# Experts' loop of a DeepNorm encoder layer: every engine held to program order, with splits, sums and weights laid out in a software pipeline

## The chip, the cores and the metric

One core of a Trainium2 chip runs the whole kernel. The metric is the time of one execution on the device in microseconds (us), lower is better. PE (TensorE) multiplies, DVE (VectorE) and ACT (ScalarE) work on tiles, POOL (GpSimd) issues DMAs and small copies, SP (SyncE) issues DMAs.

## What is computed

One encoder layer over 512 positions of 2048 features: adaptive modulation, two kinds of attention, and a retrieval of experts (PEER). The change touches the last part alone:

```python
def peer(h, wq, keys, u_tab, v_tab):            # tables: 16384 experts x 2048
    ...                                          # 8 heads choose 16 experts each: et, gt
    a = jnp.einsum('td,thkd->thk', xt, u_tab[et])
    w = gt * jax.nn.gelu(a, approximate=False)
    return jnp.einsum('thk,thkd->td', w, v_tab[et])
...
x = layer_norm(DN_ALPHA * x + g2 * p, ln2_g[l], ln2_b[l])
```

## The kernel before

Each of the 512 positions takes 128 of the 16384 experts, and the kernel computes this in two ways side by side. For 352 positions (TD, the matmul's columns) it goes densely through all experts: **u product** of a block of 128 experts (16 row blocks of the table, 3 matmuls each since every operand is split into a high and a low half of reduced precision: 48 matmuls), Gelu, times the dense weights, then **v product** into 16 sums of 128 x 352 (accT in SBUF). For the other 160 positions it gathers rows: one indirect DMA brings 128 rows of 2048 values (1 MB, a *row* tile), DVE multiplies and sums it (L1058 for u, L1064 for v).

Experts come in 32 groups of 4 blocks (GE = 4). The u products of 56 blocks are made in the stages before; their Gelu values lie in DRAM (ga_d). The experts' loop then runs over n = 0 to 18: for group gorder[n] (14 to 31) it makes the 4 u products, and between them the 4 v products (j = 0 to 3, 512 output features each) of the group before it: "u, v, u, v, ...". This is the **u/v part**. After it the v products of groups 0 to 13 remain (the **v-only part**, code under the pool "fin"); the last, 13, has another shape and flows into the final normalization. Between the two lies the **transition**: gate2 is spread to rows (`row_into`, L285 to L290), the norm's gain and bias are loaded, and group 0's weights are made.

The tables' pieces (128 x 1024, 512 KB) stream through SP's queue. `Stream._load` issues raw loads 6 pieces ahead, `Stream.fill` splits 3 pieces ahead: whi on ACT (L99), wlo on DVE (L100). A u product uses two pieces, a v product two. There are five buffers of each.

A v product (`v_mm`) has four units, dd = 0 to 3. A unit copies its sum from accT into one of six PSUM banks (o; ACT, L1157), adds 12 matmuls (L1164 to L1166), and copies the bank back (ACT, L1168). Its weights W are made by `weigh`: a product gl x gt on DVE (L1138), hi half on ACT (L261), lo half on DVE (L253). gt, 704 KB of dense weights per group, comes by a POOL DMA (L1133); gl is the Gelu's result, in the v-only part loaded by POOL from ga_d (L1288).

`step` after every product sends gathered rows on their way: per u/v pair about 3. A row is stamped by POOL with a value of the newest wlo (`paced`, L296, so that it is not issued too early), its indirect DMA is issued (L1083), and the row two before it is used (LAG = 2). There are three row buffers.

What sets the order: a scheduler arranges each engine's instructions, apart from those that `pin` or `keep_in_program_order` holds to the order of the code. `pin` acts as long as `inorder[0]` is true; it is set false long before the experts' loop, so there only the rows' uses on DVE (L1058, L1064) are held to program order. Splits, copies, matmuls, POOL's issues and SP's loads are placed by the scheduler. On each engine instructions run in the order placed.

## Time and profile before

| | us |
|---|---|
| median of 3 runs (lowest to highest) | 3654.53 (3647.95 to 3659.76) |
| the profiled execution's own time | 3652.83 |
| its span in the trace | 3650.3 |
| u/v part, transition, v-only part | 2028 to 3130, 3130 to 3210, 3210 to 3591 |

The profile was taken on an execution of 3652.83 us; the trace's span leaves out 2.5 us of start and end. Times in the trace count from the start of the span. An instruction runs when its engine has come to it in order and all that it needs is there; what it waited for last is shown as its releaser. A row of a window gives the engines' busy times and instruction counts in that stretch, the granted clock of TensorE (1.00 is full speed), and what the DMA engines did.

### The profile page before, as it was taken

The page shows a single profiled execution, that of the slowest core. Times are in us where ns is not written, and L with a number is a line of the kernel's source. Part 1 is how long each engine was busy: PE and PEld are TensorE (multiplying, and loading weights), DVE is VectorE, ACT ScalarE, POOL GpSimd, SP SyncE. Part 2 cuts the span into 40 slices and gives each one's busy share as a digit, 9 for nine tenths or more (in the row PEclk, how much of TensorE's full clock was granted, in tenths as well). Part 3 has the DMA queues.
Part 4 walks back from the last instruction along what each step waited for, and adds up shares of the span by engine and source line. Part 5 has one row for each costly group of instructions (what it writes and reads, how often), then busy time and mean ns, then how long its engine had stood idle before and what let it go on. Part 6 is the DMA issues. An engine that isn't in the chain of part 4 may idle for free. (4 is left out here: it accounts for less than half of the span.)

```text
span 3650.3 us, 52934 instructions
## 1 busy us (share of the span) xinstructions
PE 3564.6 (98%) x20127; PEld 3285.3 (90%) x20127; DVE 2700.8 (74%) x3754; ACT 1755.3 (48%) x3072; POOL 912.9 (25%) x1068
## 2 busy tenths in 40 slices
PE   8999999999999999999999999999999999899998
PEld 6888888887787889999999999999999999899997
DVE  8757587545555769988888677877877887777786
ACT  3233332233333455445666345555455555577774
POOL 0001110012120000003322333434434343434331
PEclk9999999999999999999999999999999999999999
DMA  9746488744357664446998999999989899999983
GB/s 393 260 165 228 162 298 317 254 140 124 116 193 244 203 202 157 128 132 226 344 343 343 328 345 342 342 339 342 352 336 345 340 349 347 335 358 339 352 335 122
DMA packets 216207, 996.72 MB, mean 273 GB/s; under 512 B 26816, under 2 KB 34160, under 8 KB 159344
## 3 DMA queue, kind: packets, MB, share of 16 engines
q1 hardware_dynamic: 131904, 525.93, 40.4%
q0 software_dynamic: 73104, 431.48, 31.9%
q10 hardware_dynamic: 10944, 35.94, 2.6%
q8 instruction: 157, 2.57, 0.3%
q14 instruction: 98, 0.80, 0.1%
HBM read 930.42 MB, written 61.51 MB: 272 GB/s over the span
## 5 line engine op out<-in xcount | busy, mean ns | idle before, releaser
L100 DVE TENSOR_TENSOR wlo<-raw,whi 128x1024 fp32r<-128x1024 f32 x800 | 971.7, 1221 | 543.5 <-ACT whi L99 337.9
L99 ACT ACTIVATE whi<-raw 128x1024 fp32r<-128x1024 f32 x800 | 836.3, 1055 | 824.2 <-PE main L162 493.1
L159 PE MATMUL q<-dh,whi 128*128 128x352 f32 x1680 | 546.7, 325 | 2.0 <-ACT glf L926 1.3
L163 PE MATMUL q<-dh,wlo 128*128 128x352 f32 x1680 | 542.5, 324 | 2.1 <-DVE wlo L100 2.0
L162 PE MATMUL q<-dl,whi 128*128 128x352 f32 x1680 | 543.1, 323 | 0.0
L296 POOL COPY row<-wlo 128x1 f32<-128x1 f32 x320 | 167.8, 525 | 896.3 <-DVE row L1058 404.3
L1168 ACT ACTIVATE accT<-o 128x352 f32<-128x352 f32 x480 | 216.7, 461 | 320.0 <-PE o L1166 318.6
L159 PE MATMUL main<-hh,whi 128*128 128x512 f32 x912 | 352.7, 393 | 11.4 <-ACT hh L354 11.2
L162 PE MATMUL main<-hl,whi 128*128 128x512 f32 x912 | 356.4, 391 | 0.0
L163 PE MATMUL main<-hh,wlo 128*128 128x512 f32 x912 | 348.7, 392 | 0.0
L159 PEld LDWEIGHTS q<-dh,whi 128*128 128x128 f32 x1680 | 316.6, 188 | 3.1 <-ACT glf L926 1.6
L163 PEld LDWEIGHTS q<-dh,wlo 128*128 128x128 f32 x1680 | 316.6, 189 | 3.2 <-DVE wlo L100 3.0
L162 PEld LDWEIGHTS q<-dl,whi 128*128 128x128 f32 x1680 | 317.8, 189 | 0.0
L1058 DVE SCALAR_TENSOR_TENSOR row<-row,h2g 128x2048 f32<-128x2048 f32 x128 | 291.8, 2285 | 19.2 <-DMA row<-in_peer_u,gidx 19.0
L1064 DVE SCALAR_TENSOR_TENSOR h2g<-row,au,h2g 128x2048 f32<-128x2048 f32 x127 | 298.0, 2347 | 6.4 <-DMA row<-in_peer_v,gidx 5.9
L300 DVE SCALAR_TENSOR_TENSOR adaw<-adaw,cond 128x2048 f32<-128x2048 f32 x96 | 218.5, 2288 | 99.9 <-DMA adaw<-in_w_ada_t 96.2
L159 PE MATMUL main<-qh,whi 128*128 128x352 f32 (+2 forms) x752 | 242.8, 323 | 7.4 <-ACT qs L950 7.4
L163 PE MATMUL main<-qh,wlo 128*128 128x352 f32 (+2 forms) x752 | 242.7, 323 | 0.0
L162 PE MATMUL main<-ql,whi 128*128 128x352 f32 (+2 forms) x752 | 242.0, 322 | 0.0
L1083 POOL DMA_INDIRECT row<-in_peer_v,gidx x128 | 216.1, 1688 | 41.9 <-POOL row L296 36.0
L1157 ACT ACTIVATE o<-accT 128x352 f32<-128x352 f32 x480 | 217.4, 468 | 6.0
L159 PEld LDWEIGHTS main<-hh,whi 128*128 128x128 f32 x912 | 172.1, 189 | 48.8 <-ACT hh L354 12.8
(1358 smaller groups left out, 8048.9 us busy)
## 6 DMA issues: line engine op xcount, KB each, us to landing
raw<-in_wst SPq DMA_DIRECT2D x288, 512.0 KB, 4.2
raw<-in_u_t SPq DMA_DIRECT2D x256, 512.0 KB, 6.8
raw<-in_v_t SPq DMA_DIRECT2D x256, 512.0 KB, 7.2
adaw<-in_w_ada_t SPq DMA_DIRECT2D x96, 1024.0 KB, 7.1
g_d<-stg ACTq DMA_DIRECT2D x11, 2048.0 KB, 10.6
gt<-g_d POOLq DMA_DIRECT2D x18, 704.0 KB, 11.0
ga_d<-glf ACTq DMA_DIRECT2D x56, 176.0 KB, 4.2
gl<-ga_d POOLq DMA_DIRECT2D x56, 176.0 KB, 7.4
```

The costliest lines, as they stand in the source:

```text
L99: self.nc.scalar.activation(hi, raw, AF.Copy)
L100: self.pin(self.nc.vector.tensor_tensor(out=lo, in0=raw, in1=hi.bitcast(F32), op=ALU.subtract))
L159: op = nc.tensor.matmul(ps, lh, rh, start=first, stop=False)
L162: nc.tensor.matmul(ps, lh, rl, start=False, stop=False)
L163: nc.tensor.matmul(ps, ll, rh, start=False, stop=last)
L296: eng.tensor_copy(t[:, 0:1], src.bitcast(F32)[:, 0:1])
L300: pin(nc.vector.scalar_tensor_tensor(w, w, 1.0, cond, op0=ALU.mult, op1=ALU.mult, accum_out=mod[:, j : j + 1]))
L1058: op = nc.vector.scalar_tensor_tensor(row, row, 1.0, h_, op0=ALU.mult, op1=ALU.mult, accum_out=a_[:, c : c + 1])
L1064: op = nc.vector.scalar_tensor_tensor(accs[n], row, a_[:, c : c + 1], accs[n], op0=ALU.mult, op1=ALU.add)
L1083: nc.gpsimd.indirect_dma_start(out=row, out_offset=None, in_=src, in_offset=off)
L1157: nc.scalar.activation(o, sum_, AF.Copy)
L1168: nc.scalar.activation(sum_, o, AF.Copy)
```

## The change

`pin` gets levels. At `inorder[0] = 2`, from the beginning of the experts' loop to group 13, it holds to program order: the matmuls of u and v products, whi, wlo, SP's loads, the copies to and from the banks, Gelu, the parts of the weights, POOL's stamps, and POOL's DMAs for rows, gt and gl. The code is rewritten into the order wanted: the sums' copies into PSUM are issued four units ahead (`copy_in(u + 4)` after unit u is copied out; the six banks stay). The weights' two steps, product and hi/lo pair, are carried out by `v_mm` after its units 0 and 1 (`beside`). At n = 18, in place of a u product, one gl of group 0 is loaded (POOL) and its weights are made beside the v product. In the v-only part `first_w(g + 1)` issues gt and four gl one group ahead, and their weights are made beside the products of group g.

```diff
-            self.nc.scalar.activation(hi, raw, AF.Copy)
+            self.pin(self.nc.scalar.activation(hi, raw, AF.Copy), 2)
...
+        pin(nc.tensor.matmul(ps, lh, rh, start=first, stop=False), 2)
...
-    inorder = [True]
+    inorder = [1]
...
+    def pin(op, level=1):
+        if inorder[0] >= level:
             tc.keep_in_program_order(op)
...
-                paced(row, None, nc.gpsimd)
+                pin(paced(row, None, nc.gpsimd), 2)
...
+        def product():
+            v3 = gl.rearrange("p (t c) -> p t c", t=NCH)
+            pin(nc.vector.tensor_tensor(out=v3, in0=v3, in1=gt[:, :, j, :], op=ALU.mult), 2)
+        def pair():
+            pin(nc.scalar.activation(hi, gl, AF.Copy), 2)
+            pin(nc.vector.tensor_tensor(out=lo, in0=gl, in1=hi.bitcast(F32), op=ALU.subtract), 2)
+        return [product, pair]
...
+    def copy_in(u):
+        if 16 <= u < nunits:
+            pin(nc.scalar.activation(ob_[u % 6][:, :TD], accT[:, u % 16], AF.Copy), 2)
...
-            if not start:
-                nc.scalar.activation(o, sum_, AF.Copy)
...
+            copy_in(u + 4)
+            if beside:
+                beside.pop(0)()
+        for f in beside:
+            f()
...
+    inorder[0] = 2
...
         for n in range(len(gorder) + 1):
-            if n < len(gorder):
-                gt = load_g(wk, gorder[n])
+            g = gorder[n] if n < len(gorder) else 0
+            gt = load_g(wk, g)
             for j in range(GE):
+                gl = gl_of(g, j)
                 if n < len(gorder):
                     ps = u_mm(g * GE + j)
+                    pin(nc.scalar.activation(gl, ps[:, :TD], AF.Gelu), 2)
                     step()
+                else:
+                    pin(nc.gpsimd.dma_start(gl, ga_d[j]), 2)
+                work = weigh(gl, gt, g, j)
                 if n > 0:
-                    v_mm(gorder[n - 1], j, n == 1)
+                    v_mm(gorder[n - 1], j, None, work)
                     step()
...
+        def first_w(g):
+            gt = load_g(wk, g, gts[g % 2])
+            work = []
             for j in range(GE):
                 gl = wk.tile([P, TD], F32, tag="gl", name=f"gl{g}_{j}", bufs=4)
+                pin(nc.gpsimd.dma_start(gl, ga_d[g * GE + j]), 2)
+                work.append(weigh(gl, gt, g, j))
+            return work
+        for g in range(last + 1):
+            work = first_w(g + 1) if g < last else []
...
-                    v_mm(g, j, False, mod[:, 80:96] if g == last - 1 else None)
+                    v_mm(g, j, mod[:, 80:96] if g == last - 1 else None, work[j])
```

Three places show how instructions move. The first is DVE where the u/v part begins; numbers behind names count pieces and rows. Pieces 400 and 401 belong to the loop's first u product, 402 and 403 to its second, 404 and 405 to its third. Before:

```order
L1058 SCALAR_TENSOR_TENSOR row47_17648,au_10953<-row47_17648,h2g_14371 128x2048
L100 TENSOR_TENSOR wlo403_18090<-raw403_17949,whi403_18089 128x1024
L100 TENSOR_TENSOR wlo404_18120<-raw404_17991,whi404_18119 128x1024
L1058 SCALAR_TENSOR_TENSOR row48_17716,au_10953<-row48_17716,h2g_14371 128x2048
L100 TENSOR_TENSOR wlo405_18162<-raw405_18021,whi405_18161 128x1024
L1058 SCALAR_TENSOR_TENSOR row49_17720,au_10953<-row49_17720,h2g_14371 128x2048
```

After:

```order
L1058 SCALAR_TENSOR_TENSOR row47_17648,au_10953<-row47_17648,h2g_14371 128x2048
L1058 SCALAR_TENSOR_TENSOR row48_17716,au_10953<-row48_17716,h2g_14371 128x2048
L1058 SCALAR_TENSOR_TENSOR row49_17720,au_10953<-row49_17720,h2g_14371 128x2048
L1058 SCALAR_TENSOR_TENSOR row50_17910,au_10953<-row50_17910,h2g_14371 128x2048
L1058 SCALAR_TENSOR_TENSOR row51_17978,au_10953<-row51_17978,h2g_14371 128x2048
L1058 SCALAR_TENSOR_TENSOR row52_17982,au_10953<-row52_17982,h2g_14371 128x2048
L100 TENSOR_TENSOR wlo403_18091<-raw403_17949,whi403_18090 128x1024
L100 TENSOR_TENSOR wlo404_18121<-raw404_17991,whi404_18120 128x1024
```

Rows 48 to 52 now stand ahead of wlo403.

The second is ACT in the steady u/v part, from the sums of the first product of group 23 to the second Gelu of group 24; o695 to o700 are the six banks. Before:

```order
L1168 ACTIVATE accT_18064<-o696_18078 128x352
L1157 ACTIVATE o696_18078<-accT_18064 128x352
L1168 ACTIVATE accT_18064<-o697_18079 128x352
L1157 ACTIVATE o697_18079<-accT_18064 128x352
L1168 ACTIVATE accT_18064<-o698_18080 128x352
L1157 ACTIVATE o698_18080<-accT_18064 128x352
L1168 ACTIVATE accT_18064<-o699_18081 128x352
L1157 ACTIVATE o699_18081<-accT_18064 128x352
L99 ACTIVATE whi560_23895<-raw560_23796 128x1024
L1206 ACTIVATE gl24_1_23925<-q783_23864 128x352
L99 ACTIVATE whi561_23940<-raw561_23802 128x1024
L99 ACTIVATE whi559_23865<-raw559_23751 128x1024
```

After:

```order
L1184 ACTIVATE accT_18064<-o695_18077 128x352
L1162 ACTIVATE o699_18081<-accT_18064 128x352
L1184 ACTIVATE accT_18064<-o696_18078 128x352
L1162 ACTIVATE o700_18082<-accT_18064 128x352
L1145 ACTIVATE W24_0h_23791<-gl24_0_23720 128x352
L1184 ACTIVATE accT_18064<-o697_18079 128x352
L1162 ACTIVATE o695_18077<-accT_18064 128x352
L1184 ACTIVATE accT_18064<-o698_18080 128x352
L1162 ACTIVATE o696_18078<-accT_18064 128x352
L99 ACTIVATE whi559_23870<-raw559_23756 128x1024
L99 ACTIVATE whi560_23900<-raw560_23797 128x1024
L1230 ACTIVATE gl24_1_23868<-q742_23869 128x352
```

The copy in (L1157, now L1162) goes to the bank four units on, no longer to the one just emptied; the hi half stands between two units, and the splits follow their numbers.

The third is POOL where the u/v part ends; gl0_0 to gl0_3 are group 0's Gelu values, ga_d their place in DRAM. Before:

```order
L296 COPY row256_28162<-wlo674_28101 128x1
L1288 DMA gl0_0_28800<-ga_d0_162 128x352
L1288 DMA gl0_1_28807<-ga_d1_163 128x352
L1288 DMA gl0_2_28814<-ga_d2_164 128x352
L1288 DMA gl0_3_28821<-ga_d3_165 128x352
L1083 DMA row256_28162<-in_peer_v,gidx_10951 128x2048
```

After:

```order
L1233 DMA gl0_0_28472<-ga_d0_162 128x352
L296 COPY row264_28547<-wlo684_28483 128x1
L1083 DMA row264_28547<-in_peer_v,gidx_10951 128x2048
L1233 DMA gl0_1_28551<-ga_d1_163 128x352
L296 COPY row265_28626<-wlo686_28562 128x1
L1083 DMA row265_28626<-in_peer_v,gidx_10951 128x2048
L296 COPY row266_28630<-wlo686_28562 128x1
L1083 DMA row266_28630<-in_peer_v,gidx_10951 128x2048
L1233 DMA gl0_2_28634<-ga_d2_164 128x352
L296 COPY row267_28709<-wlo688_28645 128x1
L1083 DMA row267_28709<-in_peer_v,gidx_10951 128x2048
L1233 DMA gl0_3_28713<-ga_d3_165 128x352
```

The four loads of gl that stood together now stand one per product: the first directly behind group 0's gt, the others behind a row or two each.

## Rows read from the trace of the kernel before

**Rows 1.** The page: busy time, share of the span, instructions.

```profile
PE 3564.6 (98%) x20127; PEld 3285.3 (90%) x20127; DVE 2700.8 (74%) x3754; ACT 1755.3 (48%) x3072; POOL 912.9 (25%) x1068
```

**Rows 2.** Busy time by stretches: u/v part, transition, v-only part, a dense piece.

```profile
core 0: us, PE busy (x) PEld busy (x) DVE busy (x) ACT busy (x) POOL busy (x), PEclk, DMA share, GB/s
2028.00:3130.00 1102.00, 1082.11 (x6692) 1075.00 (x6692) 858.73 (x741) 553.14 (x950) 452.40 (x435) 0.99 0.92 343
3130.00:3210.00 80.00, 68.79 (x390) 64.49 (x388) 54.83 (x55) 45.83 (x90) 37.26 (x42) 0.94 0.93 342
3210.00:3591.00 381.00, 376.96 (x2344) 374.55 (x2343) 304.35 (x269) 275.17 (x536) 137.88 (x162) 1.00 0.90 335
2805.00:2870.00 65.00, 65.00 (x409) 64.96 (x407) 50.82 (x36) 34.98 (x62) 29.22 (x26) 1.00 0.94 360
```

**Rows 3.** PE's waits, u/v part: line, releaser, us, times, longest.

```profile
PE o L1166 <- DVE wlo L100: 9.0, 8, 2.1
PE o L1164 <- ACT whi L99: 7.6, 5, 2.9
```

**Rows 4.** PE's waits in the transition.

```profile
PE o L1166 <- DVE wlo L100: 6.9, 2, 6.1
...
PE q L289 <- DVE rowb L285: 1.4, 1, 1.4
```

**Rows 5.** Busy time of 4 us behind two of the longer waits.

```profile
2404.00:2408.00 4.00, 4.00 (x16) 4.00 (x15) 3.72 (x5) 0.93 (x2) 0.46 (x3) 0.50 0.92 336
...
3164.00:3168.00 4.00, 4.00 (x15) 4.00 (x15) 3.92 (x3) 0.00 (x0) 2.28 (x3) 0.50 0.99 407
3168.00:3172.00 4.00, 4.00 (x22) 4.00 (x21) 2.01 (x5) 0.46 (x1) 2.22 (x2) 0.77 1.02 371
```

**Rows 6.** Groups by line, 2028 to 3594: busy, mean ns; idle before.

```profile
L100 DVE TENSOR_TENSOR wlo<-raw,whi 128x1024 fp32r<-128x1024 f32 x392 | 475.1, 1223 | 275.0 <-ACT whi L99 73.6 <-POOL row L296 57.3 <-issue 45.0
L99 ACT ACTIVATE whi<-raw 128x1024 fp32r<-128x1024 f32 x392 | 405.7, 1051 | 51.3 <-PE q L162 16.1 <-PE o L1165 15.5 <-DMA raw<-in_u_t 14.4
...
L1064 DVE SCALAR_TENSOR_TENSOR h2g<-row,au,h2g 128x2048 f32<-128x2048 f32 x127 | 298.0, 2347 | 6.4 <-DMA row<-in_peer_v,gidx 5.9
...
L1168 ACT ACTIVATE accT<-o 128x352 f32<-128x352 f32 x480 | 216.7, 461 | 320.0 <-PE o L1166 318.6
...
L1083 POOL DMA_INDIRECT row<-in_peer_v,gidx x128 | 216.1, 1688 | 41.9 <-POOL row L296 36.0 <-issue 2.2 <-DMA row<-in_peer_v,gidx 1.9
...
L1138 DVE TENSOR_TENSOR gl<-gl,gt 128x352 f32<-128x352 f32 x72 | 37.4, 520 | 31.6 <-ACT gl L1206 31.6
```

**Rows 7.** Time line at the loop's start: the first matmul; POOL's row issues.

```profile
2027.81 0.43 PE L159 MATMUL q<-dh,whi 128*128 128x352 f32 x1 [1.34 <-ACT glf L926]
...
2016.77 0.96 POOL L1083 DMA_INDIRECT row<-in_peer_u,gidx  x1 [0.27 <-POOL row L296]
...
2018.21 0.96 POOL L1083 DMA_INDIRECT row<-in_peer_u,gidx  x1 [0.27 <-POOL row L296]
...
2024.29 1.57 POOL L1083 DMA_INDIRECT row<-in_peer_u,gidx  x1 [0.53 <-POOL row L296]
```

**Rows 8.** DMA issues, 2010 to 2060: kind, number, median us to landing.

```profile
row<-in_peer_u,gidx POOLq DMA_INDIRECT x7, 11.9
```

**Rows 9.** DMA issues, u/v part (KB each where they are equal).

```profile
gt<-g_d POOLq DMA_DIRECT2D x18, 704.0 KB, 11.0
row<-in_peer_v,gidx POOLq DMA_INDIRECT x96, 8.8
```

**Rows 10.** The row tiles' own view, 2028 to 3500.

```profile
DMA to landing us min/median/max: 5.4/8.8/15.7
```

**Rows 11.** DMA issues, 3120 to 3160.

```profile
gl<-ga_d POOLq DMA_DIRECT2D x8, 176.0 KB, 8.0
...
row<-in_peer_v,gidx POOLq DMA_INDIRECT x5, 12.8
```

**Rows 12.** DMA issues, 3210 to 3500.

```profile
gl<-ga_d POOLq DMA_DIRECT2D x37, 176.0 KB, 6.8
```

More of the change, by code (lines that the diff above doesn't have):

```diff
@@ L1082, in gather @@
                 src = a["peer_u"] if w == "u" else a["peer_v"]
-                nc.gpsimd.indirect_dma_start(out=row, out_offset=None, in_=src, in_offset=off)
+                pin(nc.gpsimd.indirect_dma_start(out=row, out_offset=None, in_=src, in_offset=off), 2)
                 rows_in.append((gitems[i], row))
@@ L1132, in load_g, with v_mm @@
             gt = wk.tile([P, NCH, GE, TG], F32, tag="gt", name=f"gt{g}", bufs=2)
-        nc.gpsimd.dma_start(gt, g_d[:, :, g * GE : (g + 1) * GE, :])
+        pin(nc.gpsimd.dma_start(gt, g_d[:, :, g * GE : (g + 1) * GE, :]), 2)
         return gt
     def weigh(gl, gt, g, j):
-        v3 = gl.rearrange("p (t c) -> p t c", t=NCH)
-        nc.vector.tensor_tensor(out=v3, in0=v3, in1=gt[:, :, j, :], op=ALU.mult)
-        W[g, j] = split_to(ww, gl, "W", TD, name=f"W{g}_{j}")
+        hi, lo = W[g, j] = [ww.tile([P, TD], F32R, tag="W" + n, name=f"W{g}_{j}{n}") for n in "hl"]
+        def product():
[5 more added lines that the diff above has]
+        return [product, pair]
     banks("peer", q=2, o=6)
     ob_ = [bank("o") for _ in range(6)]
-    no = [0]
+    nu = [0]
+    nunits = 16 * (len(gorder) + NF // GE - 1)
     def o_bank():
-        no[0] += 1
-        return ob_[no[0] % 6]
-    def v_mm(g, j, start, by=None):
+        nu[0] += 1
+        return ob_[(nu[0] - 1) % 6]
+    def copy_in(u):
+        if 16 <= u < nunits:
+            pin(nc.scalar.activation(ob_[u % 6][:, :TD], accT[:, u % 16], AF.Copy), 2)
+    def v_mm(g, j, by=None, beside=()):
         v = [st.get("v", g, j, x) for x in range(2)]
+        beside = list(beside)
         for dd in range(4):
+            u = nu[0]
+            o = o_bank()[:, :TD]
             sum_ = accT[:, j * 4 + dd]
-            o = o_bank()[:, :TD]
-            if not start:
-                nc.scalar.activation(o, sum_, AF.Copy)
             for x in range(GE):
@@ L1282, in start_sum @@
             return o
-        for g in range(last + 1):
+        def first_w(g):
             gt = load_g(wk, g, gts[g % 2])
+            work = []
             for j in range(GE):
                 gl = wk.tile([P, TD], F32, tag="gl", name=f"gl{g}_{j}", bufs=4)
-                nc.gpsimd.dma_start(gl, ga_d[g * GE + j])
-                weigh(gl, gt, g, j)
+                pin(nc.gpsimd.dma_start(gl, ga_d[g * GE + j]), 2)
[3 more added lines that the diff above has]
+            work = first_w(g + 1) if g < last else []
             if g == 0:
@@ L1299, in tile_encoder_layer @@
                 gathered()
+            if g == last:
+                inorder[0] = 0
             for j in range(GE):
                 if g < last:
-                    v_mm(g, j, False, mod[:, 80:96] if g == last - 1 else None)
+                    v_mm(g, j, mod[:, 80:96] if g == last - 1 else None, work[j])
                     if g < VN:
```

39 lines of the change are left out of this document (18 added, 21 removed).

## Prediction

> **What bounds the kernel now.** I read the page's engines first: PE is busy for 98% of the span [rows 1]. So the change can only win what PE loses inside the experts' loop, from 2028 us to about 3591 us, and the second view is there to measure that loss: the busy time by stretches [rows 2]. Its fourth row, 65 us without a break in the v-only part, is the yardstick: 65.00 us for 409 matmuls, one of which is cut by the edge, so 65/408 = 0.160 us for one of 352 columns. What a stretch is longer than its count times 0.160 us is lost, through waits and through a lower clock together: u/v part 1102.0 - 6692 x 0.160 = 31.3 us; transition 80.0 - 390 x 0.160 = 17.6 us; v-only part 381.0 - 2344 x 0.160 = 6.0 us. Together **54.9 us**, 1.5% of the span, and no edit of this kind can give more.
>
> The third view says what PE waited for. In the u/v part [rows 3] it is splits: the first whi of a product (7.6 us) and the wlo behind it (9.0 us), in waits of 1 to 3 us; in the transition one wait for a wlo is most of it [rows 4], with the turning of gate2 into rows (rowb) beside it. Order is at fault, not speed: one u and one v product take 96 x 0.160 = 15.4 us, and in that time ACT owes four whi of 1.05, four sums of 0.46 and their four copies in, a Gelu and a hi half, taken like a sum: 4.2 + 10 x 0.46, 9 us; DVE owes four wlo of 1.22, three rows of 2.35, a product of 0.52 and a lo half like it, 13 us [rows 6]. Both fit. In the order printed above, whi559 stands behind 560 and 561 although it is needed before them, and a sum's copy in stands directly ahead of the unit that needs it.
>
> These two explain 17 of the 31 us. Most of the rest is clock: after the longer waits 4 us hold 15 or 16 matmuls where 25 belong, at a granted clock of 0.50 [rows 5], half of full speed, so 1.2 GHz in place of 2.4, after PE had stood idle. Some 10 matmuls x 0.16 = 1.6 us go, and where the next 4 us are still short, 2 us. So a wait of 2 us or more costs 1.1 to 2 us on top.
>
> **The change part by part.** The base is the profiled execution, 3652.8 us, span 3650.3; it lies 1.7 us under the median of the runs.
>
> *Splits in order, copies four units ahead, weights beside products (u/v part).* Nothing is added to PE. Each wlo is due a split lead ahead: the second piece of a v product can be done three wlo (3.7 us) into a pair and is needed after the u product and six matmuls (8.6), so 5 us of cover lie beneath it. The copies in cost nothing as long as ACT runs four units (4 x 12 x 0.160 = 7.7 us) ahead. The weights' product waits for a Gelu and a gt; gt takes 11.0 us to land [rows 9] and is needed about 9.6 us into its group (a u product of 7.7 and a unit of 1.9), so once a group DVE may stand 1 to 3 us, inside those 5. That would empty the 31.3 us, were it not for the new coupling: with the splits held in program order between the rows, a row that lands late holds the wlo behind it. The chain on DVE runs: end of a wlo, POOL's stamp and the gap to the issue 0.7 (0.53 of it in [rows 7]), landing 8.8 [rows 9], use 2.35 and two wlo 2.45, that is 14.3 us, against 15.4 for the pair in which it must close. 1.1 us of slack a pair, on top of the 5. Landings reach from 5.4 to 15.7 us [rows 10]: one of 15.7 is 6.9 late and just breaks through. I leave two such waits of 2 us with 1 us of clock each: **6 us**. Bounds: 0 (none breaks through) and 31 (all that is lost now).
>
> *The start of the loop.* Here the price is known best. Before, wlo403 and 404 run as soon as they can. After, rows 48 to 52 stand ahead of wlo403. POOL issues rows 48, 49 and 50 at 2016.8, 2018.2 and 2024.3 [rows 7]; rows issued there land after 11.9 us [rows 8], so at 2028.7, 2030.1 and 2036.2. DVE uses 48 until 2031.0, 49 until 2033.4, 50 until 2038.5. Row 51 takes the buffer of 48: issue 2031.7, landing at 8.8 us 2040.5, used until 2042.9. Row 52 follows 49: issue 2034.1, landing 2042.9, used until 2045.2; wlo403 is done at 2046.4. PE begins the first product of the loop at 2027.8, after a wait of 1.3 us for a Gelu [rows 7] that stands behind a whi of 1.05 and now comes some 0.7 us earlier: from 2027.1 it needs wlo403 after one product and a half, 72 x 0.160 = 11.5 us, at 2038.6. Stall 7.8 us, and 2 us of clock: **10 us**. Bounds: with landings of 5.4 us throughout, row 52 is used by 2036.7 and nothing waits, 0; with 11.9 for rows 51 and 52 too the stall is 11, with clock 13. I take the middle, since 8.8 is the median of the whole part.
>
> *The transition.* Its largest wait, 6.9 us, goes. New is that group 0's four gl are each issued by POOL inside their own product's turn, behind a row, or two, and its stamp (order of POOL above). gl lands after 8.0 us here [rows 11], product and hi half add 1.0, and ACT, held to program order, takes no further sum out until it has the hi half. The units whose copies are already in last until 6 x 1.92 = 11.5 us after the product begins. The first gl stands directly behind gt and comes in time. The second stands behind one row: an issue of 1.7 us [rows 6], the stamp, and the row use of 2.35 that frees the buffer: 8.0 + 1.0 + 0.6 + 4.5 = 14.1, 3 us late. The third and fourth stand behind two rows and one; each inherits part of the lateness ahead: 5 and 4. The block of gate2's rows adds four ACT copies ahead of all sums of a product: 4, besides the 1.4 for which PE waits for them now [rows 4]. Clock after three or four such waits 5. Sum 3 + 5 + 4 + 4 + 1.4 + 5 = **22 us**, against 17.6 now. Bounds: 4 (only the row block and its own work) and 40 (each gl 3 us later still, as the rows in this window that take 12.8 us [rows 11] instead of 8.8 suggest).
>
> *The v-only part.* The gl of group g+1 are issued one group ahead, but their first weights are due inside the first product of group g: the product after unit 0, the hi half after unit 1, and ACT's sums behind that. gt's issue and gl's 1.7 us, landing 6.8 [rows 12], product and hi half 1.0, a sum out and a copy in 1.0: 10.5 to 11 us against the 11.5 to which the six banks reach. Half a microsecond is left at the median, so about half of 13 groups lose 1 or 2 us: 9. At two of them (groups 2 and 7) a step with two rows stands ahead of the issues on POOL: 3 more. **12 us**, against 6.0 now; bounds 3 and 45 (next section).
>
> Sum: 6 + 10 + 22 + 12 = 50 us lost, against 54.9 now. 3652.8 - 54.9 + 50 = **3648 us**. The gain of 25 us in the steady part is paid back at the three seams.
>
> One page bears against two of these terms. The Trainium skill, "DMA: Bandwidth & Descriptors", section "Anatomy of one DMA — SWDGE (gpsimd) path", fits a POOL transfer at 2.0 us plus bytes over 436 GB/s: an estimated 4.4 us for a row of 1 MB and 2.4 for a gl. By it nothing would wait at the start or at the seams and the first rival below would be the result. The trace does not agree: no row landed in under 5.4 us, the median is 8.8 [rows 10], and gl took 6.8 to 8.0 [rows 11, 12], with the queues full.
>
> **Rivals.** *A, the in-order program gets most of what is lost.* Rows and gl land early more often than late, because loads issued strictly in order of use collide less. Then the start loses 5 (half-way to no stall), u/v 3, the transition 10, the v-only part 5: 23 us. 3652.8 - 54.9 + 23 = 3621. For it: 0.5 us of margin in the v-only part cuts both ways, and short landings of 5.4 exist. Against it: the loop's queues carry 335 to 343 GB/s throughout [rows 2], so a median will not move much.
>
> *B, slower: the row chain becomes the pace.* It closes in 14.3 us at a landing of 8.8; the point from which it decides is a mean landing of 8.8 + 1.1 = 9.9 us. The mean may well lie over the median, since the tail goes to 15.7 [rows 10]; at 10.4 us each of 72 pairs takes 0.4 us too long, 29 us. In place of the u/v part's 6 that gives 3648 - 6 + 29 = 3671, and with six waits' worth of clock some 3677. For it: seven rows at the start took 11.9 [rows 8]. Against it: the 5 us of cover are spent first, and short landings refund.
>
> *C, slower: the v-only part waits once a group.* If a gl lands 2.5 us later than 6.8, half of which the transition's 8.0 shows, each of 13 groups stands 2 us and loses 1.1 in clock: 13 x 3.1 = 40 in place of 12, 3676; the transition's three gl, late by as much and with their clock, add some 12: 3688.
>
> That the change does not do what it says has no chance of its own: the order printed above shows each move on the engines.
>
> **How the numbers follow.** Forecast 0.40, with a range of its own of 3644 to 3662; A 0.34; B 0.16; C 0.10. A measurement of this kernel can tell about 0.3%, 11 us, from no change: between 3643.5 and 3665.5 is the same. So faster 0.34, same 0.40, slower 0.26. A spreads from about 3605 to 3640, B from 3668 to 3690; the range from 3610 to 3685 leaves some 0.06 below and 0.12 above.
>
> **What would show it.** Right: in the profile after, waits for splits in the steady u/v part add up to under 10 us; one wait of 6 to 9 us for a wlo stands near 2039 us at L161, just behind rows 51 and 52 on DVE; the transition shows PE waiting for copies or sums that stand behind a hi half which waited for a gl; the clock falls to half there and nowhere else. Wrong: no wait at 2039 (landings short, A); steady waits for wlo with a landing of rows directly ahead on DVE, pair after pair (B); a wait at the first product of each v-only group (C). The step I trust least is the transition, where four small delays are added as if each came through to PE.

## The result and the profile after

The changed kernel takes 3684.63 us (median of five, 3680.53 to 3693.62) against 3652.28 (median of five, 3647.05 to 3659.76) before: the ratio is 1.0092, with a 95% interval of 1.007 to 1.0113. It is slower by 0.9%, where 3648 and "the same" were forecast; 3684.6 lies just inside the upper end of the range, 3610 to 3685, and outside the 3644 to 3662 of the forecast itself. The profiled execution took 3693.62, the highest of the five; the account that follows is of this one, and the others took 4 to 13 us less.

The first view is the one that answers to [rows 2]: busy time by stretches, cut so that each holds the same matmuls as before (columns as there: length; PE, PEld, DVE, ACT, POOL with counts; granted clock; DMA share; GB/s). The fourth line is an undisturbed piece of the u/v part.

```profile
2028.00:3119.00 1091.00, 1072.12 (x6693) 1068.68 (x6694) 873.88 (x746) 539.63 (x952) 545.58 (x448) 0.99 0.94 351
3119.00:3205.50 86.50, 72.12 (x390) 68.51 (x389) 55.91 (x52) 43.50 (x89) 24.49 (x32) 0.88 0.83 306
3205.50:3631.50 426.00, 391.44 (x2343) 387.74 (x2342) 293.24 (x267) 267.93 (x539) 117.90 (x159) 0.95 0.81 291
2200.00:2900.00 700.00, 700.00 (x4406) 700.00 (x4405) 572.51 (x496) 361.18 (x645) 346.35 (x286) 1.00 0.95 358
```

With the prediction's yardstick, length less count times 0.160 us:

| stretch | lost before | forecast | lost after |
|---|---|---|---|
| u/v part, start included | 31.3 | 16 | 20.1 |
| transition | 17.6 | 22 | 24.1 |
| v-only part | 6.0 | 12 | 51.1 |
| sum | 54.9 | 50 | 95.3 |

40.4 us more are lost, and 3652.8 + 40.4 = 3693.2 is the profiled execution's time. One stretch makes the difference. (The fourth line shows the yardstick itself to be a little long: 700 us hold 4406 matmuls, 0.1589 us each. With 0.1589 the kernel before loses 65 us, not 54.9; the differences between the two kernels stay.)

What PE waited for in nearly the same stretches of the changed kernel, up to 3100 us, from there to 3210, and behind it (line, releaser: us, times, longest):

```profile
PE q L161 <- DVE wlo L100: 8.3, 2, 7.7
PE o L1182 <- DVE wlo L100: 8.3, 6, 2.1
...
PE o L1182 <- DVE wlo L100: 8.1, 2, 7.7
PE o L1180 <- ACT o L1162: 6.7, 3, 3.3
...
PE o L1180 <- ACT o L1162: 34.2, 10, 8.7
```

The first two are the u/v part up to 3100 us: one wait of 7.7 us at its start, and short ones of which five fall into 3000 to 3100 us; from 2100 to 3000 us PE does not stand at all, where the kernel before had 16 of the 17 us of [rows 3]. The next two are the transition. The last is the v-only part: ten waits for a sum's copy, 34.2 us, where the kernel before had 1.0 us of such waits. The u/v part cut once more, and below it the start of the kernel before:

```profile
2028.00:2150.00 122.00, 111.23 (x663) 109.78 (x664) 91.08 (x89) 43.88 (x70) 55.20 (x52) 0.94 0.92 340
2150.00:3000.00 850.00, 850.00 (x5348) 849.72 (x5346) 693.83 (x594) 439.02 (x782) 423.00 (x348) 1.00 0.94 357
3000.00:3119.00 119.00, 110.89 (x685) 109.17 (x686) 88.97 (x65) 56.73 (x102) 67.37 (x49) 1.00 0.90 323
```
```profile
2028.00:2150.00 122.00, 120.73 (x749) 120.07 (x749) 86.07 (x87) 49.56 (x81) 49.08 (x48) 1.00 0.92 331
```

By the yardstick 15.9 us are lost up to 2150 us (2.2 in the kernel before), nothing up to 3000 (that stretch is 5.7 us shorter than the yardstick has it), and 9.4 from there on.

**The start** has the wait that was worked out. DVE's time line of the changed kernel (start, length, line, operation, idle before and releaser) shows rows 48 to 52 one after the other, each as it lands, and wlo403 behind the last; PE's wait ends with it:

```profile
2029.72 2.29 DVE L1058 SCALAR_TENSOR_TENSOR row<-row,h2g 128x2048 f32<-128x2048 f32 x1 [4.76 <-DMA row<-in_peer_u,gidx]
...
2044.67 2.31 DVE L1058 SCALAR_TENSOR_TENSOR row<-row,h2g 128x2048 f32<-128x2048 f32 x1 [3.28 <-DMA row<-in_peer_u,gidx]
...
2046.91 2.35 DVE L100 TENSOR_TENSOR wlo<-raw,whi 128x1024 fp32r<-128x1024 f32 x2
...
2048.18 0.66 PE L161 MATMUL q<-dh,wlo 128*128 128x352 f32 x1 [7.67 <-DVE wlo L100]
```

The wait is 7.67 us, 7.8 was expected. That it fits so well is partly luck: it began at 2040.5 us, not at 2038.6, and ended at 2048.2, not at 2046.4, and the two errors cancel. The start as a whole costs more than the 10 us forecast: 15.9 against 2.2, with two short waits behind the long one (0.9 and 0.7 us) and a granted clock of 0.94 over the 122 us.

**The v-only part** did not go as worked out. One group's start, from POOL's, DVE's, ACT's and PE's time lines:

```profile
3387.89 1.12 POOL L1133 DMA_DIRECT2D rb<-g_d  x1
3389.00 2.20 POOL L1319 DMA_DIRECT2D gl<-ga_d  x4
...
3399.45 0.53 DVE L1142 TENSOR_TENSOR gl<-gl,rb 128x352 f32<-128x352 f32 x1 [10.13 <-DMA gl<-ga_d]
...
3400.01 0.50 ACT L1145 ACTIVATE W_0h<-gl 128x352 fp32r<-128x352 f32 x1 [11.11 <-DVE gl L1142]
...
3401.27 0.66 PE L1180 MATMUL o<-W_0h,whi 128*128 128x352 f32 x1 [5.61 <-ACT o L1162]
```

POOL issues gt and right behind it four gl. gl takes 10.4 us to land, DVE stands 10.1 us at the product, ACT 11.1 us at the hi half with all sums behind it, the six banks run out, and PE stands 5.6 us; the clock is at 0.57 in the 4 us that follow:

```profile
3402.00:3406.00 4.00, 4.00 (x16) 4.00 (x16) 4.00 (x4) 3.32 (x6) 0.34 (x1) 0.57 0.15 34
```

The gl tiles' own view from 3210 us on says that this is the rule: landing minimum, median, maximum, before and after.

```profile
DMA to landing us min/median/max: 4.5/6.8/10.1
```
```profile
DMA to landing us min/median/max: 8.3/10.6/12.3
```

In the kernel before, gt and the first gl of a group did not leave together; one group's on POOL:

```profile
3237.45 1.12 POOL L1133 DMA_DIRECT2D rb<-g_d  x1 [2.33 <-DVE gl L1138]
...
3245.68 1.17 POOL L1288 DMA_DIRECT2D gl<-ga_d  x2 [4.49 <-DVE W_0l L253]
```

The last and longest wait, 8.7 us at 3575, is another one: ACT comes to the store of the gathered positions, which waits for their normalization on DVE, and the splits stand behind it.

```profile
3571.11 1.54 ACTq L1276 DMA_DIRECT2D out_dram<-h2g  x2
3572.69 2.00 ACT L99 ACTIVATE whi<-raw 128x1024 fp32r<-128x1024 f32 x2 [12.73 <-DVE h2g L1273]
```

### The profile page after: what moved, and what is told of

Same layout as the page of the kernel before. It is cut to its first block, busy times and chain, and to the rows that moved or that the text cites. A ratio compares the mean times of both kernels' runs of the same rounds, so it can differ in the third digit from the quotient of the medians.

```text
span 3690.7 us, 52903 instructions
## 1 busy us (share of the span) xinstructions
PE 3571.6 (97%) x20127; PEld 3295.0 (89%) x20127; DVE 2703.5 (73%) x3754; ACT 1728.9 (47%) x3072; POOL 968.2 (26%) x1068
## 5 line engine op out<-in xcount | busy, mean ns | idle before, releaser
L100 DVE TENSOR_TENSOR wlo<-raw,whi 128x1024 fp32r<-128x1024 f32 x800 | 961.0, 1223 | 329.9 <-ACT whi L99 325.0
L99 ACT ACTIVATE whi<-raw 128x1024 fp32r<-128x1024 f32 x800 | 822.5, 1055 | 779.2 <-PE main L160 499.2
L296 POOL COPY row<-wlo 128x1 f32<-128x1 f32 x320 | 276.5, 864 | 958.8 <-DVE wlo L100 766.6
L159 PE MATMUL main<-hh,whi 128*128 128x512 f32 x912 | 352.9, 393 | 10.4 <-ACT hh L354 10.2
L1162 ACT ACTIVATE o<-accT 128x352 f32<-128x352 f32 x480 | 223.7, 466 | 0.0
L1180 PE MATMUL o<-W_0h,whi 128*128 128x352 f32 x496 | 164.1, 331 | 40.9 <-ACT o L1162 40.9
## 6 DMA issues: line engine op xcount, KB each, us to landing
gl<-ga_d POOLq DMA_DIRECT2D x56, 176.0 KB, 10.4
```

The costliest lines, as they stand in the source:

```text
L99: self.pin(self.nc.scalar.activation(hi, raw, AF.Copy), 2)
L100: self.pin(self.nc.vector.tensor_tensor(out=lo, in0=raw, in1=hi.bitcast(F32), op=ALU.subtract))
L159: pin(nc.tensor.matmul(ps, lh, rh, start=first, stop=False), 2)
L296: return eng.tensor_copy(t[:, 0:1], src.bitcast(F32)[:, 0:1])
L1162: pin(nc.scalar.activation(ob_[u % 6][:, :TD], accT[:, u % 16], AF.Copy), 2)
L1180: pin(nc.tensor.matmul(o, vh[:, s], wh, start=first, stop=False, **kw), 2)
```

## The experiments

Each is the changed kernel with the edit shown; e1 to e15 are their names. None leaves out a part of the computation.

**gl and gt.** Two runs change their places on POOL's queue. In e1 the gt of the group after next follows the four gl:

```diff
+        gta = {1: load_g(wk, 1, gts[1])}
         def first_w(g):
-            gt = load_g(wk, g, gts[g % 2])
+            gt = gta.pop(g)
...
                 work.append(weigh(gl, gt, g, j))
+            if g < last:
+                gta[g + 1] = load_g(wk, g + 1, gts[(g + 1) % 2])
             return work
```

> The changed kernel, but in the v-only part gt of group g+2 is issued behind the four gl of group g+1, so a full group (about 31 us) before its use; gl, rows and everything else stay where they are. Theory Q (gl's 10.4 us are a queue behind gt: on POOL's queue a gl lands 0.5 to 1 us after the 704 KB gt issued just ahead of it): median landing of gl from 3210 us on falls from 10.5 to 7 or 8 us, the waits for copies at L1180 fall from 34 us to some 12 (the last, 8.7 us, is another matter), and the time falls by 25 to 33 us, to 3652 to 3660. Rival L (the whole DMA load of this part is what delays gl, wherever gt stands, since the same bytes move): gl still lands after 9.5 us or more, the waits stay above 25 us, the time falls by less than 8 us.

Measured 3642.97 us, ratio to the kernel before 0.9969 (0.9958 to 0.9979): 41.7 us under the changed kernel, and faster than before. The profile's DMA view for 3200 to 3560 us, PE's waits there, and the v-only part's busy times:

```profile
gl<-ga_d POOLq DMA_DIRECT2D x48, 176.0 KB, 7.2
```
```profile
PE o L1180 <- ACT o L1162: 7.6, 2, 7.3
```
```profile
3192.00:3574.50 382.50, 374.86 (x2345) 374.29 (x2344) 293.46 (x267) 270.56 (x539) 118.47 (x158) 0.99 0.88 324
```

gl lands after 7.2 us, the waits fall from 34.2 to 7.6, of which 7.3 is group 12's store. gt still takes 11 us, now with nobody waiting. Theory Q holds, L falls. More than the expected 25 to 33 us came back: the v-only part loses 7.3 us by the yardstick in e1's profile, 51.1 in the changed kernel's; 27 us of the difference are waits, and the rest is the clock, 0.95 there and 0.99 here.

e2 only swaps the two, gl ahead of gt at the same moment:

```diff
+            gls = [wk.tile([P, TD], F32, tag="gl", name=f"gl{g}_{j}", bufs=4) for j in range(GE)]
+            for j in range(GE):
+                pin(nc.gpsimd.dma_start(gls[j], ga_d[g * GE + j]), 2)
             gt = load_g(wk, g, gts[g % 2])
...
-                pin(nc.gpsimd.dma_start(gl, ga_d[g * GE + j]), 2)
-                work.append(weigh(gl, gt, g, j))
-            return work
+            return [weigh(gls[j], gt, g, j) for j in range(GE)]
```

> The changed kernel, but in the v-only part the four gl of a group are issued ahead of its gt instead of behind it, at the same moment. Theory Q: gl lands early (7 to 8 us) but gt now lands last, 11 to 13 us after the group's start, and the product needs both: waits and time as in the changed kernel, within 8 us of 3684. Rival G (it is gl's own small transfers that are slow, gt would have been there): gl early is enough, waits fall under 15 us and the time by 20 us or more.

3704.98 us (1.0136, 1.0113 to 1.0159). gl lands after 7.3 us and it does not help: the product needs both, and gt, issued 2.3 us later, lands 11.5 us after that. The waits for copies grow from 34 to 50 us. G falls; theory Q had the side right, but expected a time within 8 us of the changed kernel's, and it is 20 us more: the 2.3 us of later issue come through in good part, group after group.

**The start (e3).** The five gathers of the last stage ahead of the loop are left to the loop:

```diff
-                gather(RG * (i + 1) // UG - RG * i // UG)
+                if ch < NCH - 1:
+                    gather(RG * (i + 1) // UG - RG * i // UG)
...
-    rate = (NROW - RG * NCH) / (2.0 * GE * len(gorder) + VW * GE * VN - 2)
+    rate = (NROW - RG * (NCH - 1)) / (2.0 * GE * len(gorder) + VW * GE * VN - 2)
```

> The changed kernel without the five row gathers of the last stage ahead of the loop (they join the paced ones in the loop: 3.06 rows a pair instead of 2.99), so that on DVE wlo403 stands directly behind row 47. Theory D (the 7.7 us wait near 2048 us is DVE working off rows 48 to 52 in program order): that wait goes, no other of over 2 us takes its place before 2100 us, and the time falls by 8 to 12 us, to 3673 to 3677. Rival M (the rows only move: with more rows a pair the chain of rows is what PE then waits for): waits for wlo of 1 to 2 us appear pair after pair in the u/v part and the time falls by less than 4 us or rises.

3691.35 us (1.0104, 1.0087 to 1.012), 7 us more, not 8 to 12 less. The wait at 2048 is gone, but DVE then stands at the next thing in program order, the first weights' product, for a gt that was issued as the loop began:

```profile
2029.33 2.28 DVE L1058 SCALAR_TENSOR_TENSOR row<-row,h2g 128x2048 f32<-128x2048 f32 x1
...
2043.39 0.53 DVE L1143 TENSOR_TENSOR gl<-gl,gt 128x352 f32<-128x352 f32 x1 [11.77 <-DMA gt<-g_d]
```

PE waits 3.0, 1.6 and 1.4 us for that. From 2028 to 2150 us this kernel falls 9 us behind the kernel before, where the changed one falls 13 behind; so 4 us are won there, and lost again later, in the v-only part (50 us against 45). D is right about the wait, wrong about what is late next. These traces are of e3's fastest execution and the changed kernel's slowest; why the medians lie 7 us apart the other way they do not show.

**Normalization and store (e4)** of the gathered positions, spread over group 12's products:

```diff
-            mv = moments(wk, stts[ND], f"fmv{ND}")
-            for c in range(2):
-                cs = cols(2 * c, 2)
-                norm_rows(accg, cs, accg[:, cs], mv)
-                store(ND, accg, cs, nc.scalar)
...
+        def normed(j):
+            if j == 0:
+                for x in range(4):
+                    pin(nc.vector.bn_stats(stts[ND][:, x, :], accg[:, cols(x)]), 2)
+                x1["mv"] = moments(wk, stts[ND], f"fmv{ND}")
+            elif j < 3:
+                cs = cols(2 * (j - 1), 2)
+                norm_rows(accg, cs, accg[:, cs], x1["mv"])
+            if j > 1:
+                pin(nc.scalar.dma_start(out[ND * P :, cols(2 * (j - 2), 2)], accg[:, cols(2 * (j - 2), 2)]), 2)
...
+                    if g == last - 1:
+                        normed(j)
```

> The changed kernel, but the normalization and the two stores of the 160 gathered positions, which stood in one block ahead of group 12's products (13 us of DVE, the store's issue on ACT in front of the splits), are spread over group 12's four products. Theory S (the 8.7 us wait at 3575 us is ACT held by the store and DVE by the block): that wait goes or falls under 2 us, the time falls by 8 to 11 us, to 3673 to 3677. Rival X (gl and gt of group 13, landing behind 4 MB of residual rows on POOL's queue, would have held PE anyway): a wait of 5 us or more stays at the first product of group 12 and the time falls by less than 5 us.

3670.26 us (1.0043, 1.0027 to 1.0058): 14 us less, a little more than expected, and the wait at 3575 is gone. Theory S.

**The v-only part without the order (e7).** From its beginning `inorder[0] = 0`, and each group's weights are made in one go, as in the kernel before; the copies stay four units ahead in the code:

```diff
+        inorder[0] = 0
         def first_w(g):
...
-            work = first_w(g + 1) if g < last else []
+            for f in [f for w in first_w(g) for f in w] if g else []:
+                f()
...
-                    v_mm(g, j, mod[:, 80:96] if g == last - 1 else None, work[j])
+                    v_mm(g, j, mod[:, 80:96] if g == last - 1 else None)
```

> The changed kernel up to the end of the u/v part; from there on nothing is held to program order, and a group's weights are made in one go at the start of the group, as in the kernel before. Theory V (the whole loss sits in the v-only part; u/v and start are a net gain of 12 us): 3684 - 45 = 3640, between 3634 and 3648, faster than before. Rival W (the v-only part pays for what the u/v part gained, for example by rows or loads that come later): 3655 or more.

3627.34 us (0.9928, 0.9912 to 0.9945), even less than expected: 57 us under the changed kernel and some 26 under the kernel before. Not all of the 26 us come from ahead of the v-only part, for PE has no wait in that part any more:

```profile
3181.00:3556.00 375.00, 375.00 (x2363) 375.00 (x2361) 292.58 (x267) 289.49 (x541) 140.74 (x155) 1.00 0.90 330
```

These are 0.1587 us per matmul, where the kernel before took 381 us for 2344: some 9 us are won there, and some 17 by the rest of the change. The order in the v-only part more than cancels both. W falls.

**The transition (e5).** gt one group ahead in the u/v part too, group 0's gl two products ahead:

```diff
-            gt = load_g(wk, g)
+            gt = gtn if n else load_g(wk, g)
+            if n < len(gorder):
+                gtn = load_g(wk, (gorder + [0])[n + 1])
+            else:
+                gls = [gl_of(0, j) for j in range(GE)]
+                for x in range(2):
+                    pin(nc.gpsimd.dma_start(gls[x], ga_d[x]), 2)
...
                     v_mm(gorder[n - 1], j, None, work)
+                    if n == len(gorder) and j < 2:
+                        pin(nc.gpsimd.dma_start(gls[j + 2], ga_d[j + 2]), 2)
```

> The changed kernel, but in the u/v part each gt is issued one group ahead (group 0's, too), and group 0's four gl are issued two products ahead instead of inside their own product. Theory T (the transition's waits, 7.7 + 1.3 + 2.1 us and some clock, are group 0's gt, landing after 15.8 us, and its gl): these waits go, the 3.3 us behind gate2's rows stay, the time falls by 8 to 13 us, to 3672 to 3677. Rival N (the 2.7 MB of norm gain, bias and group 1's gt that stand ahead on POOL's queue delay whatever follows): the first gl now lands late instead, waits of 8 us or more stay and the time falls by less than 4 us.

3677.46 us (1.0066, 1.0046 to 1.0087), 7 us less, between the two. The 7.7 us wait became 6.0 and stayed. POOL's and DVE's time lines of the changed kernel tell why it is neither gt nor gl:

```profile
3115.24 0.58 POOL L1251 DMA_DIRECT2D rb<-in_ln_g  x1 [2.51 <-PE q L161]
...
3118.44 2.91 POOL L1083 DMA_INDIRECT row<-in_peer_v,gidx  x1 [0.28 <-POOL row L296]
...
3136.47 2.35 DVE L1064 SCALAR_TENSOR_TENSOR h2g<-row,au,h2g 128x2048 f32<-128x2048 f32 x1 [9.79 <-DMA row<-in_peer_v,gidx]
```

Norm gain, norm bias and group 1's gt (2.7 MB) go out from 3115 us on; the row issued behind them at 3118 lands 17.9 us later, and DVE, held to program order, stands 9.8 us at it with the next wlo behind. Rival N is right on the cause, though the waits and the time fell by more than it has. The two norm loads are not pinned, and group 1's gt is pinned only behind an unpinned clearing of a tile, so that all three floated ahead; that this is the reason for the order fits the code and was not tested by itself. Group 0's gt and first gl come next and land 15 us after their issue:

```profile
gt<-g_d POOLq DMA_DIRECT2D x1, 704.0 KB, 15.8
```

**What in the change gains?** The edits of e1 and e4 together are the base, e9:

> The changed kernel with two mends only: gt one group ahead in the v-only part, and the gathered positions' norm and stores spread over group 12. If the two losses add up: 3684 - 42 - 14 = 3628, between 3622 and 3636. If the first already took most of the second (with gt ahead, group 12's wait was still 7.3 us, so it should not): 3640 or more. It is the base for the next two.

3644.44 us (0.998, 0.997 to 0.9989): nothing on top of e1, where 14 us were expected. Then the same code with the order left to the scheduler, e10:

```diff
-    inorder[0] = 2
     with pool("peer", 2, "right") as wk:
```

> The kernel of e9 with the same code, but nothing in the experts' loop held to program order (the rows' uses excepted, as before the change): the scheduler places splits, copies, matmuls and POOL's issues. Theory O (the order on the engines is what gained some 25 us in the u/v part): short waits for whi and wlo come back there, 20 us or more in all, and the time is 3648 to 3662. Rival C (the code's new arrangement, copies four units ahead and weights beside products, gains by itself, whoever sets the order): within 6 us of e9.

3647.42 us (0.9986, 0.9976 to 0.9995), 3 us above e9, which by its size is rival C; the trace says O. The waits of its u/v part are those of [rows 3], to the digit:

```profile
PE o L1182 <- DVE wlo L100: 9.0, 8, 2.1
PE o L1180 <- ACT whi L99: 7.6, 5, 2.9
```

So new code without the order gains nothing in the u/v part. The order gains 38 us between some 2110 and 3110 us (e1, e7 and e13; the starts of the matmuls around these two times against those of the same matmuls in the kernel before; e10 gains 0.6), and e9 gives that back at three places that e10 does not have: the start, the transition, and a run of waits that comes next. e9 and e10 end near each other for different reasons. And e11, e9 with the copies only two units ahead:

```diff
-            copy_in(u + 4)
+            copy_in(u + 2)
```

> The kernel of e9 with the sums copied into PSUM two units ahead instead of four, all else held to program order. Theory K (ACT's order is what counts; two units are 3.8 us, and between two sums ACT has at most two whi and a hi half, 2.6 us): within 5 us of e9. Rival B (four units are needed, because the hi half waits for a product that DVE comes to late): 10 us or more above e9, with waits for copies at L1180 spread over the whole loop.

3672.22 us (1.0049, 1.0031 to 1.0066), 28 above e9: theory K falls, and it is rival B by its size, but the waits do not lie all over the loop. They are 32.4 us from 3130 us on, 19.7 of them in the transition (one of 11.5); the steady u/v part is as in e9. Four units ahead are the cover for late weights, mostly at the seams.

**The stamps.** In the changed kernel PE waits for a wlo in five pairs in a row from 3000 to 3100 us. POOL's and DVE's time lines there:

```profile
3052.74 4.94 POOL L296 COPY row<-wlo 128x1 f32<-128x1 f32 x1 [6.08 <-DVE wlo L100]
...
3052.59 2.35 DVE L1064 SCALAR_TENSOR_TENSOR h2g<-row,au,h2g 128x2048 f32<-128x2048 f32 x1
3054.86 2.36 DVE L100 TENSOR_TENSOR wlo<-raw,whi 128x1024 fp32r<-128x1024 f32 x2
3057.13 0.52 DVE L1142 TENSOR_TENSOR gl<-gl,gt 128x352 f32<-128x352 f32 x1
3058.27 0.59 DVE L1146 TENSOR_TENSOR W_3l<-gl,W_3h 128x352 fp32r<-128x352 f32 x1 [0.63 <-ACT W_3h L1145]
```

POOL's copy of one column, 0.18 us at the shortest and 0.41 at the median of the u/v part, starts behind the wlo and lasts until 3057.7, the moment at which DVE, busy without a gap since 3048.0, pauses for the first time. The row goes out 5 us late and the next wlo with it. Stamps on DVE, e6:

```diff
-                pin(paced(row, None, nc.gpsimd), 2)
+                pin(paced(row), 2)
```

> The changed kernel, but a row's stamp (one column copied from the newest wlo) is made by DVE instead of POOL. In the changed kernel POOL's stamp takes up to 4.95 us while DVE works without a break, and five waits of 1.5 to 2.1 us for a wlo follow at 3017 to 3085 us. Theory P (long stamps lengthen the chain from wlo to row to wlo until it paces PE): those waits do not occur, and the time falls by 3 to 10 us. Rival O (they are an accident of that execution; chain and PE agree anyway): the time stays within 3 us of 3684.

3702.14 us (1.0126, 1.011 to 1.0143), 17 us more, where 3 to 10 less were expected. The u/v part has no such waits and gains 38 us between some 2110 and 3110, where the changed kernel's profile gained 29; but in the v-only part, where DVE stands at a group's first product, POOL's queue now stands behind it too: 50.8 us of waits. With stamps on DVE only in the u/v part, e13 (the flag is set from the loop's start to the pool "fin"):

```diff
-                pin(paced(row, None, nc.gpsimd), 2)
+                pin(paced(row, None, nc.vector if stamps[0] else nc.gpsimd), 2)
```

> The changed kernel with the rows' stamps on DVE in the u/v part alone; ahead of the loop and in the v-only part they stay on POOL. Theory P (long stamps on POOL, up to 4.95 us against 0.18, make runs of waits for a wlo, in some executions more than in others; they are worth some 10 us at the median): 3672 to 3678, and no waits for wlo pair after pair from 2100 to 3120 us. Rival E (the 17 us that stamps on DVE cost in the whole loop were lost in the u/v part): 3690 or more.

3691.38 us (1.0105, 1.0088 to 1.0122). By its time this is rival E's figure, but the trace does not show the loss where E puts it: PE's waits list nothing from 2100 to 3100 us, as P has it. There is no gain all the same: the transition loses 13 us more than in the kernel before (6.5 more in the changed kernel), and group 12's wait is 12.3 us (8.7 there). The changed kernel's other executions, 4 to 13 us under the profiled one, may well have had no run of waits to lose; that is argued, not shown. The same on the base of e9, whose profile has eight such waits, is e14:

```profile
PE o L1182 <- DVE wlo L100: 11.9, 8, 2.3
```

> The kernel of e9 (gt ahead, norm spread) with the stamps on DVE in the u/v part. Theory P: e9's gain over the changed kernel stopped at 40 us because its u/v part had the runs of waits (some 16 us in its profile): now 3628 to 3637, and the executions lie closer together than e9's 3639 to 3651. Rival Z (spreading the norm simply brings nothing once gt is ahead): 3641 to 3647.

3635.22 us (0.9948, 0.9931 to 0.9965), 9 under e9. Theory P, and why e9 gained nothing over e1: e1's profile has no run of waits, e9's has one; in the v-only part the norm did bring 5 us on top (e1 loses 1.4 us there against the kernel before, e9 wins 3.3). Each of these is read from one profile. All profiles together say the same of the stamps: the five with DVE's stamps in the u/v part (e6, e8, e13, e14, e15) have no run of waits and gain 37 to 38 us between some 2110 and 3110 us; of the ten ordered ones with POOL's stamps, five have none and gain as much (e1, e2, e4, e5, e7), and five have one and gain 22 to 29 (the changed kernel, e3, e9, e11, e12). So a run costs 9 to 16 us, and with POOL's stamps it comes in some executions and not in others.

**All seams mended**: e1, e3, e4 and e5, norm gain and bias in groups 1 and 2, gate2's rows a quarter per product, the first group's weights one product later; stamps on DVE (e8), on POOL (e12), on DVE in the u/v part alone (e15). The edits that no run above has:

```diff
+                    for w in [late.pop(0)] if j and j < GE - 1 else late if j else []:
+                        for f in w:
+                            f()
...
+        def row_done(j):
+            ps, b = rps[j]
+            pin(nc.tensor.matmul(ps, ones, b.rearrange("p a b -> p (a b)"), start=True, stop=True), 2)
+            pin(nc.scalar.activation(g2[:, j * 512 : (j + 1) * 512], ps, AF.Copy), 2)
...
-        row_into(wk, g2, mod, 80, "rowb", "q")
...
+            if g in (1, 2):
+                ln_rows(*((l2g, "ln2_g"), (l2b, "ln2_b"))[g - 1])
```

> The changed kernel with every seam mended: gt one group ahead in both parts, norm and stores of the gathered positions spread, group 0's gl two products ahead, gate2's rows made one quarter per product of the last u/v group, norm gain and bias loaded in groups 1 and 2, the stamps on DVE, no gathers in the last stage ahead of the loop, and the first group's weights made one u product later. Theory (the losses measured one by one add up): 42 (gt) + 14 (norm) + 10 (transition) + 8 (start) = 74 us under 3684, so 3605 to 3620. Rival (the seams hide one another, and some 20 us come back as other waits, above all late rows): 3630 or more.

> The kernel of e8 with the rows' stamps back on POOL. The stamps on DVE alone made the changed kernel 17 us slower, with waits in the v-only part up from 34 to some 60 us. Theory E (a stamp on DVE stands behind the weights' product there, and holds POOL's queue with the row behind it): 3600 to 3609, faster than e8's 3612. Rival F (with gt ahead no product waits any more, so the place of the stamp is of no account): within 4 us of 3612, or above.

> The kernel of e8 (all mended) with the stamps on DVE in the u/v part, on POOL in the v-only part. The v-only part lost 1.4 us against the kernel before with stamps on DVE (e8) and won 2.9 with stamps on POOL (e12), the u/v part won 33 and 15. Theory P + E: the better of both, 3605 to 3610. Rival: nothing is left in the v-only part, 3610 to 3615.

| | us | ratio to before |
|---|---|---|
| e8, stamps on DVE | 3612.02 | 0.9887 (0.987 to 0.9903) |
| e12, stamps on POOL | 3628.84 | 0.9943 (0.9929 to 0.9956) |
| e15, both | 3609.18 | 0.9881 (0.9864 to 0.9897) |

E falls as a whole (the waits of e6 that it starts from were 50.8 us, not some 60): with the seams mended the stamp's place in the u/v part is worth 20 us (e12 against e15; 14 of them between some 2110 and 3110 us in the profiles), its place in the v-only part 3 at most (e8 against e15, not clear of the noise). e12 has the runs of waits again (2780 to 2834 and 3084 to 3118 us). e15 beats both kernels, by 43 and 75 us. Its stretches, cut like the others:

```profile
2028.00:3101.00 1073.00, 1066.64 (x6681) 1064.74 (x6680) 892.40 (x960) 537.62 (x949) 461.60 (x235) 1.00 0.95 357
3101.00:3171.00 70.00, 67.13 (x393) 64.00 (x392) 56.18 (x57) 44.09 (x91) 28.43 (x26) 0.98 0.88 329
3171.00:3545.00 374.00, 373.90 (x2343) 373.57 (x2342) 290.05 (x264) 266.98 (x535) 118.88 (x161) 1.00 0.90 335
```

4.0 and 7.1 us are lost by the yardstick, and nothing in the v-only part, where PE has no wait: the loads are those of the changed kernel, and none comes too late.

## Why the prediction was wrong, point by point

- **The base and the ceiling** held: 54.9 us were said to be there to win, 65 by the better yardstick (65/408 is 0.1593, and was rounded up), and e15 won 43 at the median.
- **The steady u/v part** was right in its main point, that the order takes the scattered waits out: from 2150 to 3000 us nothing is lost. The 6 us that were left in the sum, two rows landing too late, did not come. What came in their place is a run of waits at the end, 9.4 us in the profiled execution, from POOL's stamp, which the sum took at 0.7 us with its issue and which took up to 4.95.
- **The start** was right in its wait (7.8 forecast, 7.67 measured, with two errors that cancel) and too cheap in its price (10 forecast, 15.9 measured).
- **The transition** had the right sum (22, measured 24.1) from partly wrong terms. Its longest wait, 7.7 us, is a row behind 2.7 MB of other loads, not the gl that the sum was made of. The first gl, which "stands directly behind gt and comes in time", does not: gt and gl land 15 us after their issue there.
- **The v-only part** is the step that failed: 12 us forecast with a bound of 45, 51.1 measured. The step put "landing 6.8" [rows 12] into a chain in which gl is issued directly behind gt. That median came from another place in the queue: before, POOL's gl waited for their buffers, which the lo halves of the weights ahead set free, and for rows, and the first of a group was issued 2.8 to 15.4 us after gt (8.2 in the group above), when part of gt or all of it had been moved. Directly behind gt they land when gt has landed, 10.6 us. The chain of 10.5 to 11 us becomes 14 to 15, against 11.5 of cover: 3 us late. Nine groups wait for it, 0.5 to 5.6 us each, and the clock is low behind them (0.57 in the row above); without the cause (e1) the part loses 7.3 us in place of 51.1. The prediction's own [rows 9] had gt at 11.0 us. 0.5 us of margin was too little to be read off a median of other conditions.
- **Group 12's store** (8.7 us of wait, 14 with its clock by e4) was not in the sum at all: an instruction not pinned, among pinned ones, on ACT.
- **Rival C** named this: one wait per group in the v-only part, 40 us there; e1 gives back 44. It was given 0.10, with gl 2.5 us late; it is 3.8 late. That its 3688 is so near to 3684.6 is partly luck: the 12 us that it adds in the transition did not come (24.1 against 22), while group 12's store and the start cost more. The weight it needed stood in the edit printed ahead of the prediction's own sum, where `first_w` issues gt and the four gl side by side.
- The Trainium skill, "DMA: Bandwidth & Descriptors", section "Two DMAs through the same engine are not ordered", says that descriptors within one queue of one DMA engine start in order, but are pipelined. The runs agree with the first half: a gl's landing goes from 10.6 to 7.3 us when gt no longer stands ahead of it.

## What to carry to other kernels

A landing time belongs to a place in a queue. When an edit issues a small transfer behind a large one, price the small one at the large one's landing, and put what is needed first, or a full stage earlier: here one load moved was worth 42 us. Order held on every engine takes out scattered waits, but makes each late arrival stop all that stands behind it, so its price is at the seams: go through what each engine meets first there, unpinned instructions included, before trusting the gain in the middle.

## What the runs showed of the hardware

A POOL copy of 128 single values took between 0.18 and 4.95 us, and which it was went with what DVE did. The changed kernel's stamps on POOL and e8's on DVE (minimum, median, maximum in ns):

```profile
L296 POOL COPY row<-wlo x213: 177/413/4948, 2032.1 to 3126.7; 128x1 f32<-128x1 f32 x107
```
```profile
L296 DVE COPY row<-wlo x160: 144/153/156, 2101.6 to 2896.0; 128x1 f32<-128x1 f32 x160
```

From 2028 to 3640 us of the changed kernel, 95 of the 97 copies under 0.3 us start in a gap of DVE. All 77 of over 1 us end with an instruction of DVE, 41 of them where DVE then pauses; the one shown above ends within 0.1 us of DVE's first gap, behind four instructions without one. This agrees with the Trainium skill, "SBUF — State Buffer", section "SBUF: two separate sides": DVE, in an instruction with two SBUF inputs, and a GpSimd instruction that reads SBUF take one shared pair of ports under an exclusive lock, and the loser waits for the whole instruction. Here it lost to four instructions in a row: the row's use, two wlo and the product in the lines above.
